# Prompt retention of a two-layer decoder step: four key blocks against all later queries, or two chunks of 256 tokens joined by a partial state

## The chip, the cores and the metric

The kernel runs on one core of one Trainium2 chip. The metric is the device time of one execution in microseconds (us). The time before is 2185.27 us, the median of 3 runs (2183.65 to 2187.77). Engines are named as in the profile: PE is TensorE, DVE is VectorE, ACT is ScalarE, POOL is GpSimd, SP is SyncE, whose queue starts nearly all DMA transfers.

## The reference, cut to what matters

Each of two layers projects 512 prompt tokens and 64 sample tokens, runs a retention mixer of 4 heads (256 wide) and a pooling mixer of 4 groups, and projects the result out. The change lies in the retention of the prompt, which the reference computes by chunks, with a state S between them:

```python
def retention_chunk(qc, kc, vc, S, log_g):
    ...
    scores = jnp.einsum('bqhd,bkhd->bhqk', qc, kc) * dmask[None]
    intra = jnp.einsum('bhqk,bkhe->bqhe', scores, vc)
    q_decay = jnp.exp((idx + 1.0)[:, None] * log_g[None, :])
    inter = jnp.einsum('bqhd,bhde->bqhe', qc, S) * q_decay[None, :, :, None]
    k_decay = jnp.exp((C - 1.0 - idx)[:, None] * log_g[None, :])
    S_new = jnp.exp(C * log_g)[None, :, None, None] * S + jnp.einsum(
        'bkhd,bkhe->bhde', kc * k_decay[None, :, :, None], vc)
    return intra + inter, S_new
```

The chunk length does not change the result. The final state of each head is an output (new_ret_p, 256 KB per head).

## The kernel before, in words

All large products are made in three passes: an operand is split into a high and a low part (`split`, L89: ACT casts the high part at L91, DVE subtracts it at L92), and `mm3` (L116) issues high x high, high x low and low x high as L117, L118 and L119.

One layer's `in_phase` (L497) runs `head(h)` for h = 0 to 3 (L588) and then four `pool_group`s (L706). In layer one it lies at about 286 to 700 us of the span, in layer two at about 1369 to 1780 us; a head takes some 72 us. Everywhere in it PE has one filler: `columns()` (L500) computes pairs of 128-row column blocks of the input projection by `gemm` (L130). Such a gemm is 48 matmuls of 288 columns (L137) into two PSUM tiles named `acc`; the pool has four `acc` tiles, so the gemm after the next reuses the tiles of this one, and may start when DVE has added them to `part` (L512, two instructions per gemm, one per tile). The weights of a gemm come as a 1 MB transfer `raw` (L103, SP, two buffers) and are split by L91 and L92.

In a head, q and k are rotated and split, v is transposed to token-major (`token_major`, L570, transposes L577). Then, for each block j of 128 keys, the scores of all queries that may see it go into a `pb` tile (L625), DVE multiplies by the decay mask (L629), the product is split (L631), and six matmuls add it into the outputs `po[0]`, `po[1]` (L633). The width n is 512, 384, 256 and 256 columns for j = 0 to 3, because the start column is `min(j, 2) * P`. ACT copies the outputs out (L637). Then comes the part of the 64 sample tokens: `retention_state` (L375) loads 8 states of 256 KB, four of them into the ring `s0_ring` of four buffers (L380, L379), and its first matmul (L385) waits for all four loads of its group; L402 and L403 update and store these states. Head normalisation follows: `rsqrt` (L311), whose last PE step spreads a row over partitions (L327), whose copy is L328, and the multiplications L668. Only then is the final prompt state made: k is transposed with decay (L670), 24 matmuls of 256 columns (L674) fill `sf`, ACT copies it to `so`, a buffer of `s0_ring` (L676, L677), and SP stores it (L678). The gate multiplies the head's result (L681); `block_sums` (L190 to L193) and splits (L92) prepare operands that POOL's queue writes out and, from L698, reads back (`m<-operand`).

A pool group works on DVE with window scans (L730) and their corrections (L732 to L737), multiplies gates (L528) and scales (L750).

The order of instructions on each engine is set by the scheduler when the kernel is built; each engine then runs its list in that order, and semaphores hold an instruction until its inputs and buffers are ready.

Of the kernel before, what the change touches and what calls it, by code (L numbers as in the profile page):

```python
# [8 lines left out]
F32R = mybir.dt.float32r  # L9
I32 = mybir.dt.int32  # L10
AF = mybir.ActivationFunctionType
ALU = mybir.AluOpType
PSUM = bass.MemoryType.PSUM

P = 128
L = 2
KT = 16
NP = 512
# [6 lines left out]
DK = 256  # L25
# [13 lines left out]
def decoder_kernel(ctx: ExitStack, tc: tile.TileContext, a, decay8):  # L39
    nc = tc.nc  # L40
# [20 lines left out]
    def tmp():  # L61
        return buf("tmp")
# [53 lines left out]
    def mm3(out, wh, wl, xh, xl, start, stop, **kw):  # L116
        nc.tensor.matmul(out, wh, xh, start=start, stop=False, **kw)  # L117
        nc.tensor.matmul(out, wh, xl, start=False, stop=False, **kw)  # L118
        nc.tensor.matmul(out, wl, xh, start=False, stop=stop, **kw)  # L119
# [4 lines left out]
    def mix_tile():  # L124
        return ps.tile([P, 512], F32, tag="po", name="po", bufs=2)

    def bank(shape):
        return ps.tile(list(shape), F32, tag="pb", name="pb", bufs=2)
# [233 lines left out]
    consts = {}  # L362
# [134 lines left out]
    def in_phase(l, raws, r2, rB, cos, sin):  # L497
        b_ring, st_ring, rot_ring, s0_ring = Ring(0, 12), Ring(12, 4), Ring(16, 8), Ring(24, 4)
# [89 lines left out]
        def head(h):  # L588
            ident = consts["ident"]
            mask = buf("mask", (P, 640))  # L590
            nc.sync.dma_start(out=mask, in_=a["mask_p"][:, h])
            q = rotary(8 + h)
            qs = split_prompt(q)
# [7 lines left out]
            k = rotary(12 + h)  # L601
# [6 lines left out]
            vt = token_major(v)  # L608
# [8 lines left out]
            nc.scalar.copy(vs, tp[:, :DK])  # L617

            po = [mix_tile() for _ in range(2)]
            for j in range(4):  # L620
                c0 = min(j, 2) * P
                n = NP - c0
                sp = bank((P, 512))
                for dt in range(2):
                    mm3(sp[:, :n], ks[dt][0][:, j * P:(j + 1) * P], ks[dt][1][:, j * P:(j + 1) * P],  # L625
                        qs[dt][0][:, c0:], qs[dt][1][:, c0:], dt == 0, dt == 1)
                m0 = c0 - j * P + P
                sm = tmp()
                nc.vector.tensor_tensor(out=sm[:, :n], in0=sp[:, :n], in1=mask[:, m0:m0 + n], op=ALU.mult)  # L629
                sth, stl = st_ring.tile((P, NP), F32R), st_ring.tile((P, NP), F32R)  # L630
                split(sth[:, :n], stl[:, :n], sm[:, :n])  # L631
                for e in range(2):
                    mm3(po[e][:, c0:], vt[j][0][:, e * P:(e + 1) * P], vt[j][1][:, e * P:(e + 1) * P],  # L633
                        sth[:, :n], stl[:, :n], j == 0, j == 3)
            o = [rot_ring.tile() for _ in range(2)]
            for e in range(2):
                nc.scalar.copy(o[e][:, :NP], po[e])  # L637
# [29 lines left out]
            for e in range(2):  # L667
                nc.vector.tensor_tensor(out=o[e], in0=o[e], in1=ro, op=ALU.mult)  # L668

            kt = token_major(k, scale=consts["kdec"][:, h])  # L670
            sf = bank((P, 2, DK))
            for dt in range(2):
                for j in range(4):
                    mm3(sf[:, dt], kt[j][0][:, dt * P:(dt + 1) * P], kt[j][1][:, dt * P:(dt + 1) * P],  # L674
                        vt[j][0], vt[j][1], j == 0, j == 3)
            so = s0_ring.tile((P, 2, DK))  # L676
            nc.scalar.copy(so, sf)  # L677
            nc.sync.dma_start(out=a["new_ret_p"][l, h].rearrange("(t p) e -> p t e", p=P), in_=so)  # L678

            for i, g in enumerate(silu_gates(20 + h)):  # L680
                nc.vector.tensor_tensor(out=o[i], in0=o[i], in1=g, op=ALU.mult)  # L681
# [2 lines left out]
            both = buf("x", (P, 2, HN), F32R)  # L684
# [71 lines left out]
        for h in range(NH):  # L756
            head(h)
# [178 lines left out]
def _tables(np):  # L936
    f = np.float32
    half = DK // 2
    inv = (10000.0 ** (-(np.arange(half, dtype=f) / f(half))).astype(np.float64)).astype(f)
    pos = np.concatenate([np.arange(NP), 4096 + np.tile(np.arange(NS), NB)]).astype(f)  # L940
    ang = (inv[:, None] * pos[None, :]).astype(np.float64)
    lg = np.log(f(1.0) - f(2.0) ** (f(-5.0) - np.arange(NH, dtype=f))).astype(np.float64)
    sc = DK ** -0.5
    p = np.arange(P)
    d = (np.arange(640) - P)[None, :] - p[:, None]
    mask = np.where(d[:, None] >= 0, np.exp(np.maximum(d, 0)[:, None] * lg[None, :, None]) * sc, 0.0)
    tok = np.arange(64)
    t, b = tok % NS, tok // NS
    ds = t[None, :] - t[:, None]
    ok = (b[None, :] == b[:, None]) & (ds >= 0)  # L950
    mask_s = np.where(ok[:, None], np.exp(np.maximum(ds, 0)[:, None] * lg[None, :, None]) * sc, 0.0)
    kdec = np.exp((NP - 1 - (p[:, None, None] + P * np.arange(4)[None, None, :])) * lg[None, :, None]) * sc
    ones = np.ones((P, 1, 1))
    qdec_s = ones * np.exp((t[:NS] + 1)[None, :] * lg[:, None])[None]
    kdec_s = ones * (np.exp((NS - 1 - t[:NS])[None, :] * lg[:, None]) * sc)[None]
    w = np.array(WINDOWS)
    invcnt = ones * (1.0 / np.minimum(np.arange(16)[None, :] + 1, w[:, None]))[None]
    tables = {
        "cos": np.cos(ang), "sin": np.sin(ang), "ident": np.eye(P),
        "kdec": kdec, "qdec_s": qdec_s, "kdec_s": kdec_s,  # L960
        "mask_s": np.concatenate([np.zeros_like(mask_s), mask_s]), "mask_p": mask, "invcnt": invcnt,
    }
    return {k: np.ascontiguousarray(v.astype(f)) for k, v in tables.items()}, [float(np.exp(NS * g)) for g in lg]
# [63 lines left out]
```

## Time and profile before

| what | value |
|---|---|
| median of 3 runs | 2185.27 us (2183.65 to 2187.77) |
| the profiled execution's own time | 2186.74 us |
| its span | 2184.8 us |
| PE busy | 2168.9 us (99%) |
| DVE busy | 1726.2 us (79%) |
| ACT busy | 1063.6 us (49%) |
| granted TensorE clock | 9 tenths or more in every slice of 40 |

The profiled execution is 1.47 us above the median of the runs. Matmul ends in the trace are modelled and overlap the next start, so the time that a matmul takes from its successors is read from start to start.

### The profile page before, as it was taken

To read this page: it belongs to the slowest core of one execution; us is meant where nothing else is said; L and a number is where in the kernel's file an instruction comes from. 1 tells how busy PE (TensorE), PEld (TensorE's weight loads), DVE (VectorE), ACT (ScalarE), POOL (GpSimd) and SP (SyncE) were. 2 spreads that over 40 slices of the span, in tenths; PEclk is the share of its full clock that TensorE was granted. 3 is DMA by queue.
4 is the path that set the end of the run, shared out by engine and by line. 5 is a ranking of instruction groups with operands and counts; after the bars stand their busy time and mean duration, and the time that the engine had idled before them with its cause. 6 is when DMAs were issued, how large, how long until landed. Compare 5 with 4: busy or idle time off the path is not lost.

```text
span 2184.8 us, 42838 instructions
## 1 busy us (share of the span) xinstructions
PE 2168.9 (99%) x16716; PEld 2138.1 (98%) x16716; DVE 1726.2 (79%) x3186; ACT 1063.6 (49%) x2065; POOL 178.5 (8%) x210
## 2 busy tenths in 40 slices
PE   9999999999999999999999999999999999999998
PEld 9999999999999999999999999999999999999998
DVE  8788766677588998888887887667786889979865
ACT  5565534444434555655455554434443345566532
POOL 3000000000211111200110000000002111111000
PEclk9999999999999999999999999999999999999999
DMA  7455454565873333656544554456568743346564
GB/s 233 145 196 187 157 170 150 188 193 175 273 245 130 130 119 125 210 175 225 192 167 149 172 177 151 149 159 210 167 206 256 233 143 124 113 142 197 178 209 141
DMA packets 148202, 385.59 MB, mean 176 GB/s; under 512 B 15776, under 2 KB 54176, under 8 KB 127136
## 3 DMA queue, kind: packets, MB, share of 16 engines
q1 hardware_dynamic: 129168, 340.37, 47.4%
q0 software_dynamic: 18688, 42.48, 6.2%
q8 instruction: 131, 2.15, 0.4%
q14 instruction: 71, 0.58, 0.1%
q10 hardware_dynamic: 144, 0.02, 0.0%
HBM read 284.97 MB, written 97.84 MB: 175 GB/s over the span
## 4 chain that ended last, share of the span: by engine, by line
PE 90%; DVE 4%; DMA 3%; issue 1%; ACT 1%; SPq 0%; DVEq 0%; ACTq 0%
PE acc L137 34%; PE acc L119 13%; PE acc L118 13%; PE acc L117 13%; PE acc L233 3%; PE pb L118 3%; PE pb L119 3%; PE pb L117 3%; DMA x<-ple 2%; PE po L137 1%; DVE wl L92 1%; PE pb L401 1%; PE po L385 1%; PE pb L577 1%; PE po L327 1%
## 5 line engine op out<-in xcount | busy, mean ns | idle before, releaser
L137 PE MATMUL acc<-m,wh 128*128 128x288 f32 x3584 | 648.7, 296 | 0.0
L91 ACT CAST wh<-raw 128x512 fp32r<-128x512 f32 x567 | 350.5, 620 | 503.6 <-PE acc L137 263.6
L118 PE MATMUL acc<-m,wh 128*128 128x288 f32 x1944 | 573.1, 295 | 0.0
L117 PE MATMUL acc<-m,wh 128*128 128x288 f32 x1944 | 571.3, 295 | 0.9 <-ACT m L256 0.5
L119 PE MATMUL acc<-m,wl 128*128 128x288 f32 x1944 | 567.7, 295 | 0.7 <-DVE wl L92 0.7
L137 PEld LDWEIGHTS acc<-m,wh 128*128 128x128 f32 x3584 | 531.7, 188 | 7.0 <-issue 6.0
L92 DVE TENSOR_TENSOR wl<-raw,wh 128x512 fp32r<-128x512 f32 x567 | 401.7, 710 | 125.8 <-ACT wh L91 119.1
L137 PE MATMUL acc<-m,wl 128*128 128x288 f32 x1792 | 388.8, 295 | 0.0
L117 PEld LDWEIGHTS acc<-m,wh 128*128 128x128 f32 x1944 | 364.7, 188 | 2.1 <-ACT m L256 1.0
L118 PEld LDWEIGHTS acc<-m,wh 128*128 128x128 f32 x1944 | 365.0, 188 | 0.1
L119 PEld LDWEIGHTS acc<-m,wl 128*128 128x128 f32 x1944 | 362.8, 188 | 1.3 <-DVE wl L92 1.3
L91 ACT CAST wh<-S 128x512 fp32r<-128x512 f32 x356 | 220.6, 620 | 236.7 <-PE acc L118 149.7
L137 PEld LDWEIGHTS acc<-m,wl 128*128 128x128 f32 x1792 | 288.7, 188 | 1.1 <-issue 0.5
L92 DVE TENSOR_TENSOR wl<-S,wh 128x512 fp32r<-128x512 f32 x356 | 252.1, 709 | 23.6 <-ACT wh L91 22.4
L512 DVE TENSOR_TENSOR part<-acc,part 128x288 f32<-128x288 f32 x192 | 79.6, 451 | 84.2 <-PE acc L137 83.8
L246 POOL TENSOR_TENSOR S<-raw 128x512 f32<-128x512 f32 x45 | 77.9, 1732 | 650.9 <-DMA raw<-in_w_out 214.6
L246 DVE TENSOR_TENSOR S<-raw 128x512 f32<-128x512 f32 x133 | 93.5, 703 | 22.0 <-DMA raw<-in_w_in 18.0
L691 POOL DMA_DIRECT2D operand<-x x48 | 25.8, 538 | 972.1 <-ACT x L91 965.7
L118 PE MATMUL pb<-m,wh 128*128 128x288 f32 x324 | 95.5, 295 | 0.0
L119 PE MATMUL pb<-m,wl 128*128 128x288 f32 x324 | 95.2, 294 | 0.0
L117 PE MATMUL pb<-m,wh 128*128 128x288 f32 x324 | 95.1, 293 | 0.0
L256 ACT COPY d<-acc 128x288 f32<-128x288 f32 x228 | 86.3, 394 | 0.0
(280 smaller groups left out, 3388.9 us busy)
## 6 DMA issues: line engine op xcount, KB each, us to landing
raw<-in_w_in SPq DMA_DIRECT2D x95, 1024.0 KB, 5.4
raw<-in_w_out SPq DMA_DIRECT2D x32, 1024.0 KB, 5.1
raw<-in_w_gate SPq DMA_DIRECT2D x32, 1024.0 KB, 5.6
proj<-d SPq DMA_DIRECT2D x96, 288.0 KB, 2.1
part<-proj SPq DMA_DIRECT2D x96, 288.0 KB, 3.1
operand<-x POOLq DMA_DIRECT2D x56, 288.0 KB, 3.3
m<-operand POOLq DMA_DIRECT2D x56, 288.0 KB, 5.5
x<-in_x SPq DMA_DIRECT2D x36, 288.0 KB, 4.1
```

The lines of the kernel that those rows point to most:

```text
L91: nc.scalar.copy(hi, src)
L92: return nc.vector.tensor_tensor(out=lo, in0=src, in1=hi.bitcast(F32), op=ALU.subtract)
L117: nc.tensor.matmul(out, wh, xh, start=start, stop=False, **kw)
L118: nc.tensor.matmul(out, wh, xl, start=False, stop=False, **kw)
L119: nc.tensor.matmul(out, wl, xh, start=False, stop=stop, **kw)
L137: nc.tensor.matmul(acc[h], u, v[:, h * HN:(h + 1) * HN], start=(i == 0 and passno == 0), stop=(i == n - 1 and passno == 2),)
L233: nc.tensor.matmul(acc[h], w[:, j], xs[h][passno == 1], start=(i == 0 and j == 0 and passno == 0), stop=(i == 1 and j == 3 and passno == 2),)
L246: eng.tensor_tensor(out=s, in0=x, in1=y, op=op)
L256: ops["tail_act"] = nc.scalar.copy(dst, src)
L327: nc.tensor.matmul(rows[:, (q % 2) * QN:(q % 2 + 1) * QN], pick[:, q], r, start=True, stop=True)
L512: nc.vector.tensor_tensor(out=half(t, h), in0=acc[h], in1=half(t, h), op=ALU.add)
L691: nc.gpsimd.dma_start(out=operand_dram[l][7 * h + 1 + 2 * i + k], in_=part)
```

## The change

Prompt retention now works in two chunks of 256 tokens. Key blocks 0 and 1 meet only queries 0 to 255, blocks 2 and 3 only queries 256 to 511, so all four widths are 256. The partial state of keys 0 to 255 is made first (12 matmuls), copied by ACT into `so` and split; the queries of the second chunk are multiplied on DVE by a decay table, which lies in an unused part of the mask, and split; and 12 new matmuls of 256 columns add their product with the partial state to the outputs. The state of keys 256 to 511 (12 matmuls) is then added to `so` by DVE and stored. The whole making of the state therefore moves from behind the head normalisation to a place ahead of the sample part, and `so` takes its `s0_ring` buffer ahead of this head's four state loads. In the changed kernel the lines of the places below are 29 higher, and 20 higher from the gate multiplication on: L668 is L697 there, L681 is L701, L730 is L750, L678 is L663.

```diff
             po = [mix_tile() for _ in range(2)]
+            n = 2 * P
             for j in range(4):
-                c0 = min(j, 2) * P
-                n = NP - c0
+                c0 = j // 2 * n
+                cols = slice(c0, c0 + n)
...
-                        qs[dt][0][:, c0:], qs[dt][1][:, c0:], dt == 0, dt == 1)
+                        qs[dt][0][:, cols], qs[dt][1][:, cols], dt == 0, dt == 1)
...
-                    mm3(po[e][:, c0:], vt[j][0][:, e * P:(e + 1) * P], vt[j][1][:, e * P:(e + 1) * P],
-                        sth[:, :n], stl[:, :n], j == 0, j == 3)
+                    mm3(po[e][:, cols], vt[j][0][:, e * P:(e + 1) * P], vt[j][1][:, e * P:(e + 1) * P],
+                        sth[:, :n], stl[:, :n], j % 2 == 0, j == 1, skip_group_check=True)
+
+            kt = token_major(k, scale=consts["kdec"][:, h])
+
+            def state_of(js):
+                sf = bank((P, 2, DK))
+                for dt in range(2):
+                    for j in js:
+                        mm3(sf[:, dt], kt[j][0][:, dt * P:(dt + 1) * P], kt[j][1][:, dt * P:(dt + 1) * P],
+                            vt[j][0], vt[j][1], j == js[0], j == js[-1])
+                return sf
+
+            so = s0_ring.tile((P, 2, DK))
+            nc.scalar.copy(so, state_of((0, 1)))
+            s1h, s1l = (st_ring.tile((P, 2, DK), F32R) for _ in range(2))
+            split(s1h, s1l, so)
+            qb = []
+            for dt in range(2):
+                t = tmp()[:, :n]
+                nc.vector.tensor_tensor(out=t, in0=q[dt][:, n:NP], in1=mask[:, 3 * P:], op=ALU.mult)
+                both = st_ring.tile((P, 2, n), F32R)
+                split(both[:, 0], both[:, 1], t)
+                qb.append((both[:, 0], both[:, 1]))
+            for e in range(2):
+                for dt in range(2):
+                    mm3(po[e][:, n:], s1h[:, dt, e * P:(e + 1) * P], s1l[:, dt, e * P:(e + 1) * P], *qb[dt],
+                        False, dt == 1, skip_group_check=True)
+            nc.vector.tensor_tensor(out=so, in0=so, in1=state_of((2, 3)), op=ALU.add)
+            nc.sync.dma_start(out=a["new_ret_p"][l, h].rearrange("(t p) e -> p t e", p=P), in_=so)
...
-            kt = token_major(k, scale=consts["kdec"][:, h])
-            sf = bank((P, 2, DK))
-            for dt in range(2):
-                for j in range(4):
-                    mm3(sf[:, dt], kt[j][0][:, dt * P:(dt + 1) * P], kt[j][1][:, dt * P:(dt + 1) * P],
-                        vt[j][0], vt[j][1], j == 0, j == 3)
-            so = s0_ring.tile((P, 2, DK))
-            nc.scalar.copy(so, sf)
-            nc.sync.dma_start(out=a["new_ret_p"][l, h].rearrange("(t p) e -> p t e", p=P), in_=so)
...
     mask = np.where(d[:, None] >= 0, np.exp(np.maximum(d, 0)[:, None] * lg[None, :, None]) * sc, 0.0)
+    mask[:, :, 3 * P:] = np.exp((np.arange(2 * P, NP) - (NP - 1))[None, None, :] * lg[None, :, None])
```

The scheduler gives the changed kernel another order of instructions. Three places of it follow; a tile's name carries its buffer's number, so two rows with one number speak of one tile.

**PE at the end of the last head of a layer.** Before, the row spreading L327 stands near the end of a gemm (tiles acc_7921 and acc_7922):

```order
L137 MATMUL acc_7922<-m38_2490,wh_7917 128x288
L327 MATMUL po_7322<-tmp_7309,pick_63 128x144 x2
L327 MATMUL po_7326<-tmp_7309,pick_63 128x144 x2
L137 MATMUL acc_7921<-m39_2491,wh_7917 128x288
L137 MATMUL acc_7922<-m39_2491,wh_7917 128x288
```

Now, two matmuls into the next gemm (acc_8283 and acc_8284), with the gemm of acc_8198 and acc_8199 just finished; 46 matmuls later comes acc_8390, which takes the buffer of acc_8198:

```order
L137 MATMUL acc_8198<-m42_2790,wl_8195 128x288
...
L137 MATMUL acc_8199<-m42_2790,wl_8195 128x288
L137 MATMUL acc_8283<-m28_1740,wh_8273 128x288
L137 MATMUL acc_8284<-m28_1740,wh_8273 128x288
L327 MATMUL po_7484<-tmp_7471,pick_63 128x144 x2
L327 MATMUL po_7488<-tmp_7471,pick_63 128x144 x2
L137 MATMUL acc_8283<-m29_1741,wh_8273 128x288
...
L137 MATMUL acc_8284<-m42_2790,wl_8278 128x288
L137 MATMUL acc_8390<-m28_1740,wh_8382 128x288
```

So L327 has moved from behind the 32nd matmul of a gemm to behind the 2nd of one, as a count over the lists shows.

**DVE at the same place.** Before, the two additions L512 that free a finished gemm's tiles stand between the gate multiplications:

```order
L668 TENSOR_TENSOR m22_7187<-m22_7187,tmp_7299 128x576
L668 TENSOR_TENSOR m23_7188<-m23_7188,tmp_7299 128x576
L681 TENSOR_TENSOR m22_7187<-m22_7187,g_7444 128x576
L512 TENSOR_TENSOR part_7911<-acc_7921,part_7911 128x288
L681 TENSOR_TENSOR m23_7188<-m23_7188,g_7512 128x576
L512 TENSOR_TENSOR part_7911<-acc_7922,part_7911 128x288
L92 TENSOR_TENSOR wl_8162<-raw_7812,wh_8161 128x512
```

Now the same seventeen other instructions come first, and the two L512 after all of them (the middle of the list is left out):

```order
L697 TENSOR_TENSOR m22_7349<-m22_7349,tmp_7461 128x576
L697 TENSOR_TENSOR m23_7350<-m23_7350,tmp_7461 128x576
L701 TENSOR_TENSOR m22_7349<-m22_7349,g_7556 128x576
L701 TENSOR_TENSOR m23_7350<-m23_7350,g_7624 128x576
L190 TENSOR_TENSOR tmp_7628<-m22_7349 128x288
...
L752 TENSOR_TENSOR tmp_7738<-tmp_7734,c_invcnt_1050 128x16
L754 SCALAR_TENSOR_TENSOR tmp_7738<-tmp_7734,d_7728 128x496
L92 TENSOR_TENSOR wl_8548<-raw_8281,wh_8547 128x512
L512 TENSOR_TENSOR part_8188<-acc_8198,part_8188 128x288
L512 TENSOR_TENSOR part_8188<-acc_8199,part_8188 128x288
```

The release of acc_8198 has moved behind the start of the pool group's work (L750, L752 and L754 are its scan and corrections).

**SP in the last head.** Before, the store of a head's state and the load that reuses its buffer stand early in the following head (here the store of head 2, and its reuse by head 3):

```order
L506 DMA part<-proj_292 128x576
L678 DMA out_new_ret_p<-m_6466 128x2x256
L380 DMA m_7208<-in_state_ret 128x2x256
L506 DMA part<-proj_251 128x576
L103 DMA raw<-in_w_in 128x2048
```

Now head 3 stores its own state, and its own fourth state load reuses the buffer; a weight load stands ahead of the store:

```order
L380 DMA x<-in_state_ret 128x2x256 x4
L103 DMA raw<-in_w_in 128x2048
L663 DMA out_new_ret_p<-m_7293 128x2x256
L380 DMA m_7370<-in_state_ret 128x2x256
L403 DMA out_new_ret_s<-m_7364 128x2x256
```

The load of m_7370 is one of the four that L385 of the same head waits for. On PE, 76 matmuls of L137, 12 of the new product and eight small ones lie between the end of head 3's state matmuls and that L385. In heads 1 and 2 a weight load also stands ahead of the store, in head 0 none.

## Rows read from the trace of the kernel before

**Rows 1.** The page: the span, each engine's busy time (share of the span) and instructions, and the chain of waits by engine.

```profile
span 2184.8 us, 42838 instructions
PE 2168.9 (99%) x16716; PEld 2138.1 (98%) x16716; DVE 1726.2 (79%) x3186; ACT 1063.6 (49%) x2065; POOL 178.5 (8%) x210
PE 90%; DVE 4%; DMA 3%; issue 1%; ACT 1%; SPq 0%; DVEq 0%; ACTq 0%
```

**Rows 2.** Timeline of PE in head 0 of layer one, at the scores (first and third matmul of three in a row), and one stretch of plain gemm: start in us, time in us, engine, line, operation, out<-in, array, shape, count.

```profile
333.44 0.39 PE L117 MATMUL pb<-m,m 128*128 128x512 f32 x1
...
333.90 0.39 PE L119 MATMUL pb<-m,m 128*128 128x512 f32 x1
...
335.59 0.34 PE L117 MATMUL pb<-m,m 128*128 128x384 f32 x1
...
335.94 0.34 PE L119 MATMUL pb<-m,m 128*128 128x384 f32 x1
...
338.48 0.28 PE L117 MATMUL pb<-m,m 128*128 128x256 f32 x1
...
338.72 0.28 PE L119 MATMUL pb<-m,m 128*128 128x256 f32 x1
...
598.81 0.69 PE L137 MATMUL acc<-m,wh 128*128 128x288 f32 x4
599.34 0.42 PE L137 MATMUL acc<-m,wl 128*128 128x288 f32 x2
599.60 0.70 PE L137 MATMUL acc<-m,wh 128*128 128x288 f32 x4
```

**Rows 3.** Groups of DVE and ACT instructions between 286 and 700 us, shapes apart: line, engine, operation, out<-in, shape, count, then busy us and mean ns of one, then the idle time before them and what ended it.

```profile
L629 DVE TENSOR_TENSOR tmp<-pb,mask 128x512 f32<-128x512 f32 x4 | 2.8, 692 | 1.6 <-PE pb L119 1.6
L629 DVE TENSOR_TENSOR tmp<-pb,mask 128x256 f32<-128x256 f32 x8 | 3.4, 424 | 4.3 <-PE pb L119 4.3
L92 DVE TENSOR_TENSOR m<-m,m 128x512 fp32r<-128x512 f32 x16 | 10.6, 686 | 3.2 <-ACT m L91 3.2
L91 ACT CAST m<-m 128x512 fp32r<-128x512 f32 x16 | 9.9, 621 | 6.8 <-PE pb L119 5.2 <-DVE m L522 1.5
L677 ACT COPY m<-pb 128x512 f32<-128x512 f32 x4 | 2.3, 587 | 3.7 <-PE pb L119 3.4
```

**Rows 4.** Busy time of the engines in stretches: from:to, then length, and busy us (instructions) of PE, PEld, DVE, ACT and POOL, granted clock, DMA share, GB/s. The first lies in head 0, the second in head 3, the third in the pool groups.

```profile
340.00:344.00 4.00, 4.00 (x29) 3.83 (x27) 1.23 (x5) 1.56 (x4) 0.00 (x0) 1.00 0.40 83
556.00:564.00 8.00, 8.00 (x61) 7.82 (x60) 2.34 (x6) 1.72 (x5) 4.31 (x8) 1.00 0.99 329
600.00:616.00 16.00, 16.00 (x123) 16.00 (x122) 16.00 (x35) 7.20 (x12) 5.93 (x11) 1.00 0.79 248
```

**Rows 5.** Timeline of PE at the end of head 3, layer one and (last) layer two; columns as in rows 2.

```profile
597.30 1.15 PE L327 MATMUL po<-tmp,pick 128*128 128x144 f32 x8
598.19 0.52 PE L137 MATMUL acc<-m,wh 128*128 128x288 f32 x2
...
1680.79 1.15 PE L327 MATMUL po<-tmp,pick 128*128 128x144 f32 x8
```

**Rows 6.** Timeline of DVE there, layer one and (last two) layer two; in brackets the idle time before and what ended it.

```profile
598.91 1.43 DVE L668 TENSOR_TENSOR m<-m,tmp 128x576 f32<-128x576 f32 x2 [1.35 <-ACT tmp L328]
600.26 0.75 DVE L681 TENSOR_TENSOR m<-m,g 128x576 f32<-128x576 f32 x1
600.93 0.45 DVE L512 TENSOR_TENSOR part<-acc,part 128x288 f32<-128x288 f32 x1
601.30 0.75 DVE L681 TENSOR_TENSOR m<-m,g 128x576 f32<-128x576 f32 x1
...
608.93 0.82 DVE L512 TENSOR_TENSOR part<-acc,part 128x288 f32<-128x288 f32 x2
...
1682.40 1.43 DVE L668 TENSOR_TENSOR m<-m,tmp 128x576 f32<-128x576 f32 x2 [1.35 <-ACT tmp L328]
...
1692.42 0.81 DVE L512 TENSOR_TENSOR part<-acc,part 128x288 f32<-128x288 f32 x2
```

**Rows 7.** Transfers, each from a view of a short stretch: out<-in, queue, operation, count, KB each, median us from issue to landing. The first two are a state's store and the load that reuses its buffer, at 384 to 388 us; the next such a store at 528 to 534 us; then a weight load and the stores issued right behind it, at 357 to 360 us; then two state loads at 550 to 553 us; then head 3 at 555 to 566 us.

```profile
out_new_ret_p<-m SPq DMA_DIRECT2D x1, 256.0 KB, 2.6
m<-in_state_ret SPq DMA_DIRECT2D x1, 256.0 KB, 2.6
...
out_new_ret_p<-m SPq DMA_DIRECT2D x1, 256.0 KB, 4.1
...
raw<-in_w_in SPq DMA_DIRECT2D x1, 1024.0 KB, 6.5
out_new_ret_s<-m SPq DMA_DIRECT2D x2, 256.0 KB, 6.8
...
x<-in_state_ret SPq DMA_DIRECT2D x2, 256.0 KB, 6.9
...
m<-operand POOLq DMA_DIRECT2D x10, 288.0 KB, 5.5
x<-in_state_ret SPq DMA_DIRECT2D x1, 256.0 KB, 5.2
```

**Rows 8.** Timeline of PE in head 0: the small matmuls of the sample part; columns as in rows 2.

```profile
347.24 0.55 PE L646 MATMUL pb<-sts,vs 128*128 128x64 f32 x4
...
347.93 0.70 PE L137 MATMUL acc<-m,wh 128*128 128x288 f32 x4
```

## The prediction

> **What bounds the kernel now.** I read the page first. PE is busy 2168.9 of 2184.8 us, and the chain of waits is 90% PE [rows 1]: a PE matmul saved is time saved, and any wait put on PE is time lost, unless PE would have waited later anyway. DVE follows with 79%, which is an average. The table by stretches splits it: in the middle of a head DVE works 1.23 of 4 us, in head 3 it works 2.34 of 8 us, but at the start of the pool groups 16.00 of 16 us [rows 4]. So DVE work added in a head is cheap, and DVE work that is late at the end of a layer's last head is not. Then I read the PE timeline for the price of one matmul, the DVE timeline for the end of head 3, and the transfers, because the state's store moves.
>
> **PE columns (one answer: a gain).** A matmul's price is its start-to-start distance; modelled durations overlap. With 512 columns the first and third start 0.46 us apart, 0.23 each; with 384 it is 0.35, 0.175 each; with 256 it is 0.24, 0.12 each [rows 2]. A head loses 12 matmuls of 512 and 12 of 384, which become 24 of 256, and gains 12 of 256: 12 x 0.23 + 12 x 0.175 = 4.86 us become 36 x 0.12 = 4.32 us. That is 0.54 us a head, and for 8 heads **-4.3 us**. The state's 24 matmuls only move. This is small: the two spared blocks of scores and outputs are nearly paid back by the 12 new matmuls.
>
> The Trainium skill, "TensorE: Matmul & The Clock Gate", section on the back-to-back issue gap, speaks against the change: it gives about 81 ns per matmul at 128 columns and only about 131 ns at 512 in a stream of weight loads and matmuls. A straight line between these, an estimate from that page, gives 98 ns at 256 and 114 ns at 384, and the change would add 36 x 98 - 12 x 131 - 12 x 114 = 588 ns a head, +4.7 us in all. The rows here give 230 ns at 512, with as many weight loads as matmuls [rows 1, 2], so the measurement decides and wide matmuls are not cheap here.
>
> **DVE and ACT work in a head (nothing, by cover).** DVE adds one split of 512 columns (0.69), two decay multiplications and two subtractions of 256 (4 x 0.42) and the addition of the second half state (taken as 0.69, by the 512-wide multiplication): 3.05 us. It saves 0.27 twice for the 512-wide mask and split, and about half for the 384-wide: 0.8 us. Net +2.25 us a head [rows 3]. ACT gains some 1.1 us by the same rows. The cover is the 1.23 of 4 us [rows 4]; uncovered it would be 2.25 x 8 = 18 us, which I exclude since DVE is two thirds idle there. The 12 new matmuls wait for copy, cast and subtraction of the half state, 0.59 + 0.62 + 0.69 = 1.9 us [rows 3]; between lie, by the list of head 0, the other half's 12 matmuls (1.4 us) and 14 of the gemm's (1.8 us), so PE does not wait.
>
> **The end of head 3 (the main loss).** Here the moved order matters, and it is the longest term. Before, L512 frees the finished gemm's tiles 2.02 us after L668 starts (598.91 to 600.93) [rows 6]. In the list now, the two L512 for acc_8198 and acc_8199 stand behind seventeen instructions, starting with L697 (the old L668). These are the same seventeen that before lie between L668 and the two L512 at 608.93. So their time can be read off: 608.93 - 598.91 = 10.02 us, less two L512 at 0.37 (600.93 to 601.30) = 9.28 us; layer two gives the same 10.02 (1682.40 to 1692.42) [rows 6]. L668 starts 1.61 us after the first L327 (597.30 to 598.91; 1680.79 to 1682.40) [rows 5, 6], because it needs L328's copy. One L512 takes 0.45. The release is at 1.61 + 9.28 + 0.45 = **11.34 us** after L327 begins. PE meanwhile has the L327 group, 0.89 us (597.30 to 598.19) [rows 5], and 46 gemm matmuls at 0.132 (six from 598.81 to 599.60) [rows 2], 6.06 us: it reaches acc_8390, in the buffer of acc_8198, after **6.95 us**. It waits 4.4 us, and in two layers **+8.8 us**. The wait has no cover: the next instruction in PE's list is the one that waits, and all behind it are queued too. Ends: 0, if the release does not come last; 5.5 each, if casts on ACT hold one of the seventeen a microsecond more.
>
> What is late next is the pool groups' DVE work, which has no slack (16.00 of 16) [rows 4]. Its later releases come late by less, since PE has lost time as well. I take 0.5 us a layer, **+1.0 us**; ends 0 and 2 a layer.
>
> **The state's store, now ahead of L385.** In each head the fourth state load reuses `so`'s buffer, so it waits for the store to land, and L385 waits for the load. SP waits at that load too; queued behind it are weight and part loads, whose buffers are ahead of need. Quiet, store and load take 2.6 + 2.6 us; one such store took 4.1; stores right behind a weight load took 6.8; loads near head 3's operand reads took 5.2 to 6.9 [rows 7]. In head 3, by the list of SP, the weight load is just ahead of the store, and POOL's ten operand reads of 5.5 us fill the queues (DMA share 0.99) [rows 4, 7]. The chain is 0.69 for the addition, 6.8, and some 6.4: 13.9 us. PE has 76 gemm matmuls (10.0), 12 new ones (1.4) and eight small ones (0.69 for four by the stretch 347.24 to 347.93, 1.4 for eight [rows 8]): 12.8 us. L385 waits about 1 us; ends 0 (quiet: 5.9 us against 12.8) and 2.5 (another 1.5 us of queue). Two layers: **+2 us**. In head 0, without a weight load ahead, 0.69 + 4.1 + 2.6 = 7.4 us stays under the 8.2 us that I count for PE in the same way; heads 1 and 2 (9.0 and 7.8 us) I cost at nothing as long as the weight load has mostly passed; see the second rival.
>
> **Sum.** -4.3 + 8.8 + 1.0 + 2.0 = +7.5 us, on the profiled execution 2186.74 + 7.5 = 2194.2. That execution stands 1.47 above the median, so against the runs I predict 2185.27 + 7.5 = **2192.8 us**. A measurement of this kernel can tell some 0.2%, 4.4 us, from no change.
>
> **Rivals.**
> 1. *No wait at the end of head 3.* If the tiles come free before PE asks, and no load is late, only the columns count: 2185.3 - 4.3 = 2181.0, at the edge of faster. The place is the release of acc_8198, the price 4.4 us a layer, and the point is 6.95 us after L327: the seventeen instructions and one L512 would have to fit into 5.34 us after L697 starts. For it: the waits are inferred from a list, and such waits are scarce before. Against it: the same instructions took 9.28 us in both layers, and DVE was never idle among them.
> 2. *Loads late in heads 1 and 2 as well.* If the weight load goes out directly ahead of the store, the chain is 0.69 + 6.8 + 2.6 = 10.1 us against 9.0 and 7.8: waits of 1.1 and 2.3, 3.4 a layer, 6.8 in all, giving 2199.6. It decides by when the weight buffer comes free: 3 us before the store or at the same moment. For it: SP's list has that load directly ahead. Against it: the stores here took 2.6 and 4.1 before [rows 7].
> 3. *The wait is partly given back.* If PE, once late, spares waits that it has before, or the seventeen run shorter by what L668 waited, half of the losses go: about -4.3 + 6 = +1.7, 2187.
> 4. *The change does not narrow the work.* The list of head 0 shows the 48 matmuls at 256, the 12 new ones and the state made early, so I give this nothing.
>
> **How the numbers follow.** The forecast gets 0.55 (2190 to 2196 by itself), the second rival 0.22 (2197 to 2202), the third 0.15 (2184 to 2189), the first 0.08. The forecast and the second rival are slower by over 0.2%; the third is within 0.2%; of the first, at 2181.0 against a bound of 2180.9, I count 0.06 as faster and 0.02 as same. A small part of the forecast, 0.02, falls under the bound of 2189.6. Faster 0.06, same 0.19, slower 0.75. The range leaves out the first rival and the upper end of the second: 2184.5 to 2201.
>
> **What would show it.** Right: in the new trace, PE idles about 4.4 us before an L137 some 7 us after the last head's L327 in each layer, ended by DVE's L512; DVE starts L697 about 1.6 us after L327 and is busy without a gap until then. Score and output matmuls all stand at 0.12. DVE is still idle for much of a head. L385 of head 3 waits about 1 us for a load, of heads 0 to 2 for nothing. Wrong: PE gaps at L385 in heads 1 and 2, a gap at the 12 new matmuls, or a PE timeline without the gap after L327.

## The result: 20 us slower, and the profile after

| what | before | after |
|---|---|---|
| median, 6 runs each | 2185.28 us (2183.65 to 2188.31) | 2205.64 us (2200.28 to 2211.8) |
| ratio | | 1.0092 (95%: 1.0079 to 1.0106) |
| profiled execution, own time | 2186.74 us | 2204.03 us |

The forecast was 2192.8 us with a range up to 2201: the sign was right, the size 12.8 us too small. The page of the changed kernel, against [rows 1]:

```profile
span 2202.3 us, 43090 instructions
PE 2168.7 (98%) x16812; PEld 2142.3 (97%) x16812; DVE 1736.2 (79%) x3234; ACT 1066.4 (48%) x2089; POOL 179.5 (8%) x210
PE 82%; DMA 7%; DVE 5%; issue 4%; ACT 1%; SPq 0%; POOL 0%; DVEq 0%; ACTq 0%; POOLq 0%
```

PE's busy time is the same to 0.2 us, though its matmuls stream fewer columns, and the span is 17.5 us longer. The chain of waits has moved from PE (90% to 82%) to DMA, DVE and issue. So PE waits, and some of its matmuls take longer.

PE's timeline in the last head, both layers, answers to [rows 5] (start, time, engine, line, operation, tiles, array, shape, count, idle time before and what ended it):

```profile
580.97 0.56 PE L137 MATMUL acc<-m,wh 128*128 128x288 f32 x3
584.52 1.93 PE L385 MATMUL po<-m,u 128*32 128x256 f32 x16 [2.99 <-DMA m<-in_state_ret]
586.20 1.75 PE L385 MATMUL po<-x,u 128*32 128x256 f32 x16
587.88 0.40 PE L137 MATMUL acc<-m,wh 128*128 128x288 f32 x1
...
615.48 1.14 PE L327 MATMUL po<-tmp,pick 128*128 128x144 f32 x8
...
622.31 0.42 PE L137 MATMUL acc<-m,wl 128*128 128x288 f32 x2
626.98 0.82 PE L137 MATMUL acc<-m,wh 128*128 128x288 f32 x2 [4.24 <-DVE part L512]
627.60 0.44 PE L137 MATMUL acc<-m,wl 128*128 128x288 f32 x1
627.84 0.68 PE L137 MATMUL acc<-m,wh 128*128 128x288 f32 x2
...
1676.80 1.07 PE L385 MATMUL po<-m,u 128*32 128x256 f32 x16 [1.97 <-issue]
...
1706.40 1.14 PE L327 MATMUL po<-tmp,pick 128*128 128x144 f32 x8
...
1717.90 0.82 PE L137 MATMUL acc<-m,wh 128*128 128x288 f32 x2 [4.25 <-DVE part L512]
```

Two waits stand in each layer: one before L385 of head 3 (start to start 3.28 and 2.27 us, so some 3.15 and 2.14 us over the usual distance of 0.13), one before the L137 that reuses acc_8198's buffer, 11.5 us behind the first L327 (4.4 us each). And behind the second, one matmul takes 0.24 us (627.60 to 627.84) instead of 0.132.

DVE's timeline at the second wait, against [rows 6]:

```profile
617.09 1.43 DVE L697 TENSOR_TENSOR m<-m,tmp 128x576 f32<-128x576 f32 x2 [0.55 <-ACT tmp L328]
...
626.38 0.81 DVE L512 TENSOR_TENSOR part<-acc,part 128x288 f32<-128x288 f32 x2
```

L697 starts 1.61 us after L327 and the two L512 9.29 us after L697, as worked out (1.61 and 9.28).

The table by stretches shows what the clock did (length; busy us and instructions of PE, PEld, DVE, ACT, POOL; granted clock; DMA share; GB/s):

```profile
585.00:586.00 1.00, 1.00 (x16) 0.59 (x12) 0.00 (x0) 0.00 (x0) 0.00 (x0) 0.50 0.00 0
...
624.00:626.00 2.00, 0.00 (x0) 0.00 (x0) 2.00 (x6) 1.24 (x2) 0.98 (x2) 0.79 1.07 423
630.00:632.00 2.00, 2.00 (x10) 2.00 (x10) 1.73 (x6) 0.24 (x1) 1.54 (x3) 0.50 1.16 359
632.00:634.00 2.00, 2.00 (x17) 2.00 (x17) 1.43 (x2) 0.43 (x1) 0.80 (x2) 1.00 1.02 215
...
1676.50:1679.00 2.50, 2.20 (x34) 1.47 (x35) 1.14 (x2) 0.15 (x1) 0.00 (x0) 1.00 0.00 0
```

PE stands still, the granted clock falls from 1.00 (2.4 GHz) to 0.50 (1.2 GHz), and stays there for some microseconds after PE works again: 10 instructions in 2 us at half clock, 17 at full. The 32 L385 matmuls of head 3 take 3.36 us (584.52 to 587.88) in layer one, against 1.86 us in layer two (1676.80 to 1678.66), where the clock stood at 1.00 behind the shorter wait. The Trainium skill, "TensorE: Matmul & The Clock Gate", part 1, has the two levels and the fall after idleness; the trace agrees, at 0.50 here.

Last, the transfers of head 3, first layer one (568 to 572 us, the last row 580 to 584 us), then layer two (1660 to 1664 us, the last row 1668 to 1676 us), against [rows 7] (out<-in, queue, operation, count, KB each, median us to landing):

```profile
m<-operand POOLq DMA_DIRECT2D x6, 288.0 KB, 9.6
raw<-in_w_in SPq DMA_DIRECT2D x1, 1024.0 KB, 10.5
...
out_new_ret_p<-m SPq DMA_DIRECT2D x1, 256.0 KB, 11.4
...
m<-in_state_ret SPq DMA_DIRECT2D x1, 256.0 KB, 3.6
...
m<-operand POOLq DMA_DIRECT2D x7, 288.0 KB, 7.9
raw<-in_w_in SPq DMA_DIRECT2D x1, 1024.0 KB, 7.1
...
out_new_ret_p<-m SPq DMA_DIRECT2D x1, 256.0 KB, 8.9
...
m<-in_state_ret SPq DMA_DIRECT2D x1, 256.0 KB, 5.1
```

The state's store takes 11.4 and 8.9 us there; I had 6.8. The load that reuses its buffer, the last row of each layer, takes 3.6 and 5.1 us; I had 6.4. In layer two the profile names no releaser for the wait at L385 (`issue`), but that load was issued at 1671.61 us and landed 5.1 us later, 0.1 us before L385 starts.

**The account**, between the two profiled executions (spans 17.5 us apart): the L117 to L119 matmuls, summed from start to start over the whole trace, go from 1082.1 to 1077.9 us, -4.2. The waits behind L327 give +8.8 (2 x 4.4), those at L385 +5.3, three later waits for L512 in the pool groups +3.5 (645.08 to 646.38, 652.70 to 653.33 and 1741.43 to 1743.39 us, less 0.13 each). Two of these three hang on a `part` load for which DVE itself waits; its rows there:

```profile
645.86 0.46 DVE L512 TENSOR_TENSOR part<-acc,part 128x288 f32<-128x288 f32 x1 [1.39 <-DMA part<-proj]
...
1742.79 0.82 DVE L512 TENSOR_TENSOR part<-acc,part 128x288 f32<-128x288 f32 x2 [1.32 <-DMA part<-proj]
```

Half clock gives 1.5 (L385), 20 x 0.115 = 2.3 behind 626.98 and 12 x 0.117 = 1.4 behind 1717.90: +5.2. Together +18.6; the 1.1 us over the measured 17.5 is not traced to a place. The medians differ by 20.4, since this profiled execution is 1.6 us below its kernel's median and that of before 1.5 above.

### The profile page after: what moved, and what is told of

It reads as the page before. It is cut to its first block, busy times and chain, and to the rows that moved or that the text cites. A ratio compares the mean times of both kernels' runs of the same rounds, so it can differ in the third digit from the quotient of the medians.

```text
span 2202.3 us, 43090 instructions
## 1 busy us (share of the span) xinstructions
PE 2168.7 (98%) x16812; PEld 2142.3 (97%) x16812; DVE 1736.2 (79%) x3234; ACT 1066.4 (48%) x2089; POOL 179.5 (8%) x210
## 4 chain that ended last, share of the span: by engine, by line
PE 82%; DMA 7%; DVE 5%; issue 4%; ACT 1%; SPq 0%; POOL 0%; DVEq 0%; ACTq 0%; POOLq 0%
PE acc L137 27%; PE acc L118 13%; PE acc L117 13%; PE acc L119 13%; DMA x<-ple 4%; PE pb L119 3%; PE pb L118 3%; PE pb L117 3%; PE acc L233 3%; PE po L137 1%; DVE wl L92 1%; DVE m L882 1%; DVE x L881 1%; PE po L385 1%; DVE x L872 1%
## 5 line engine op out<-in xcount | busy, mean ns | idle before, releaser
L137 PE MATMUL acc<-m,wh 128*128 128x288 f32 x3584 | 656.6, 297 | 11.5 <-DVE part L512 11.5
L117 PE MATMUL acc<-m,wh 128*128 128x288 f32 x1944 | 571.4, 295 | 0.5 <-ACT m L256 0.5
L119 PE MATMUL acc<-m,wl 128*128 128x288 f32 x1944 | 567.4, 295 | 0.3 <-DVE wl L92 0.3
L137 PEld LDWEIGHTS acc<-m,wh 128*128 128x128 f32 x3584 | 535.9, 189 | 16.6 <-issue 13.4
L137 PE MATMUL acc<-m,wl 128*128 128x288 f32 x1792 | 401.1, 296 | 0.0
L117 PEld LDWEIGHTS acc<-m,wh 128*128 128x128 f32 x1944 | 364.6, 188 | 1.8 <-ACT m L256 1.0
L119 PEld LDWEIGHTS acc<-m,wl 128*128 128x128 f32 x1944 | 362.8, 188 | 0.8 <-DVE wl L92 0.8
L137 PEld LDWEIGHTS acc<-m,wl 128*128 128x128 f32 x1792 | 294.1, 189 | 1.3 <-issue 1.3
L512 DVE TENSOR_TENSOR part<-acc,part 128x288 f32<-128x288 f32 x192 | 79.6, 451 | 53.2 <-PE acc L137 48.6
L119 PE MATMUL pb<-m,wl 128*128 128x288 f32 x324 | 95.2, 294 | 1.5 <-DVE wl L92 1.5
L117 PE MATMUL pb<-m,wh 128*128 128x288 f32 x324 | 95.1, 293 | 0.0
```

What stands on the lines that cost most here:

```text
L137: nc.tensor.matmul(acc[h], u, v[:, h * HN:(h + 1) * HN], start=(i == 0 and passno == 0), stop=(i == n - 1 and passno == 2),)
L512: nc.vector.tensor_tensor(out=half(t, h), in0=acc[h], in1=half(t, h), op=ALU.add)
```

## The experiments

My theory, after this: the columns pay as priced, and the loss is the early state's `so` in `s0_ring`. It makes L385 wait for a store and, because the sample part and the head's end come later against the gemms, puts the head's end and the pool groups' work on DVE together, ahead of the L512 that frees PE; waits of such length then cost clock. Rival one: the added DVE and ACT work costs (2.25 us a head). Rival two: wide matmuls are cheap, so that there is nothing to gain.

**e1: so in another buffer.**

```diff
-            so = s0_ring.tile((P, 2, DK))
+            so = buf("d")[:, :2 * DK].rearrange("p (t e) -> p t e", t=2)
```

> Edit: the state buffer so comes from the ring of work buffers d, not from s0_ring; all computation is that of the changed kernel. Theory (place of so): the fourth state load no longer waits for the store of so, so L385 of head 3 has no wait (3.1 and 2.1 us go), the head's end comes earlier in the lists, the 4.4 us wait behind L327 goes in both layers, and with these waits the stretches at half clock go too. Left are the columns (-4.3) and about 1.3 us a layer of small waits for L512: 2183 to 2187 us. Rival (the added DVE and ACT work, 2.25 us a head, is what costs): the work is all still there, so the time stays near 2205, at least above 2198.

Measured: 2190.0 us (11 runs), ratio 1.0021 (1.0011 to 1.003). Three quarters of the loss went with one buffer, all the added work being still there, and in the trace no wait is left at L385 nor behind L327. The order of the matmuls shows the step between: in layer one 1874 gemm matmuls start ahead of head 3's L327 in the changed kernel, 1812 in e1 and 1760 before, so that L327 stands behind the 2nd, the 36th and the 32nd matmul of a gemm. But 2183 to 2187 was too low. PE's waits that are left in the pool groups of layer one, and the transfers at 630 to 640 us:

```profile
636.33 0.53 PE L137 MATMUL acc<-m,wh 128*128 128x288 f32 x2 [0.68 <-DVE part L512]
645.42 0.50 PE L137 MATMUL acc<-m,wh 128*128 128x288 f32 x2 [2.49 <-DVE part L512]
```

```profile
raw<-in_w_in SPq DMA_DIRECT2D x1, 1024.0 KB, 8.0
...
u<-in_state_pool SPq DMA_DIRECT2D x1, 184.0 KB, 7.9
```

The second pool group's small inputs are issued right behind a 1 MB weight load and land with it. DVE waits 2.19 us for `in_state_pool`, until 641.30, and the L512 behind that wait frees PE late. As with the state's store, a small transfer is late beside a large one, at a place I had not looked at. Behind 645.42 the clock was at half again, 15 matmuls at 0.237 (1.6 us).

**e2: the move alone, scores wide.** The whole making of the state, unsplit, stands ahead of `o`; nothing else:

```diff
+            kt = token_major(k, scale=consts["kdec"][:, h])
+            ...
+            so = s0_ring.tile((P, 2, DK))
+            nc.scalar.copy(so, sf)
+            ...
             o = [rot_ring.tile() for _ in range(2)]
```

> Edit: the kernel before with its wide scores, only with the whole making and storing of the state moved to where the change has it, so from s0_ring; no split of the state, no new matmuls, no added DVE work. Theory (the move costs): the lists again put the L512 that frees a gemm's tiles behind the last head's end; by the list it comes about 6 us late in each layer, with half clock behind it: 2185 + 12 + 4 = about 2200, 2195 to 2206. Rival (the added work costs, not the move): no work is added, so 2184 to 2188.

Measured: 2199.77 us (4 runs), ratio 1.0064 (1.0051 to 1.0078), as expected. The move costs 14 us without any added work. PE's wait, and the stretches of it and behind it:

```profile
626.42 0.82 PE L137 MATMUL acc<-m,wh 128*128 128x288 f32 x2 [6.53 <-DVE part L512]
```

```profile
619.60:626.40 6.80, 0.29 (x3) 0.06 (x2) 6.30 (x14) 2.50 (x5) 2.69 (x5) 0.89 0.97 314
626.40:631.50 5.10, 5.08 (x21) 5.10 (x22) 5.10 (x12) 1.25 (x2) 3.77 (x7) 0.50 1.14 360
```

DVE is busy through the wait (6.30 of 6.80 us), so PE waits for DVE's order, and 21 matmuls follow at half clock. This wait, its like of 6.2 us in layer two and the half clock behind both come to 18.2 us, more than the 12.4 us between the two profiled spans; where the rest is gained is not traced.

**e3: narrow columns alone.**

```diff
-                c0 = min(j, 2) * P
-                n = NP - c0
+                n = 2 * P
+                c0 = j // 2 * n
...
```

This kernel leaves out what the second chunk's queries take from the first 256 keys; it serves for the time alone.

> Edit: the kernel before, with all four widths 256 and nothing else; the second chunk's queries never meet the first 256 keys, that part of the output is left out. The state stays at its old place. Theory (columns priced from start to start): 12 x (0.23 - 0.12) + 12 x (0.175 - 0.12) = 1.98 us a head, 15.8 us in 8 heads: 2169 to 2171. Rival (wide matmuls cost little more than narrow ones, some 16 ns from 256 to 384 and 33 ns to 512): 0.6 us a head, 4.7 in all: 2180 or more.

Measured: 2171.55 us (4 runs), ratio 0.993 (0.9913 to 0.9947): 14.2 us less. From start to start, the L117 to L119 matmuls sum to 1065.5 us, 16.6 less than before; in the score, output and state matmuls alone, which hold all that the edit narrows, 69.2 against 84.9 us, 15.7 less. Rival two falls. The Trainium skill, "TensorE: Matmul & The Clock Gate", section "Back-to-back issue gap", has some 131 ns per matmul for 512 columns; the estimate from it, 4.7 us less, would have given 2180 or more, and the rows decide against it here.

**e4: the wait filled.** 32 unused matmuls between the last matmul before the wait (`last_mm`) and the one that waits:

```diff
+            if g == groups[2]:
+                fill = bank((P, 512))
+                with tc.issue_after(last_mm[0].ins):
+                    for _ in range(32):
+                        nc.tensor.matmul(fill[:, :HN], r2[1][0][:, :P], half(r2[0][0], 0), start=True, stop=True)
...
```

> Edit: the changed kernel with 32 matmuls of 288 columns, whose product nobody reads, put on PE between the last matmul before the wait behind L327 and the matmul that waits, in each layer; they need 32 x 0.132 = 4.2 us, the wait is 4.4. Theory (the slow matmuls behind the wait are the clock's, which fell because PE stood still): the wait is filled, the granted clock stays at 1.0 there, and the 20 and 12 matmuls at 0.247 us run at 0.132: 2.3 + 1.4 = 3.7 us less than the changed kernel, 2201 to 2203. Rival (they are slow because of transfers or DVE at the same place): they stay slow, 2205 to 2207. Should the filling cost time of its own, it would be 2213.

Measured: 2202.48 us (4 runs), ratio 1.0073 (1.0057 to 1.0088). PE there, and the granted clock of that stretch:

```profile
619.88 4.38 PE L734 MATMUL pb<-m,m 128*128 128x288 f32 x32
624.29 0.50 PE L139 MATMUL acc<-m,wh 128*128 128x288 f32 x2
```

```profile
626.00:628.00 2.00, 2.00 (x17) 2.00 (x16) 1.44 (x2) 0.00 (x0) 1.07 (x2) 1.00 0.47 157
```

The same matmuls, behind a wait as long but filled, run 17 in 2 us at clock 1.00, where they were 10 at 0.50. That the slowness there is the clock's is shown. The total says less: it fits 2201 to 2203, but in the trace a later wait grew to 3.04 us from start to start in layer one (1.30 in the changed kernel) and 3.00 in layer two (1.96), and behind each 25 matmuls ran at half clock. PE, earlier now, only waited later for the same DVE.

**e5: POOL's operand reads held back** until the first L385 of head 3 (`first_state`):

```diff
-                nc.gpsimd.dma_start(out=t, in_=operand_dram[l][7 * j + i])
+                after_all(nc.gpsimd.dma_start(out=t, in_=operand_dram[l][7 * j + i]), [first_state[0]])
...
```

> Edit: the changed kernel, but POOL's reads of the operands (m<-operand) wait for the first state matmul (L385) of head 3, so none of them runs while head 3's state is stored; the weight load stays right ahead of the store on SP. Behind that point the lists differ, so only the stretch up to L385 of head 3 is read. Theory (the reads make the store slow; it took 11.4 and 8.9 us): it takes 6 to 7, as stores right behind a weight load did before (6.8), the reload about 3, and the wait at L385 of head 3 is 0, at most 0.5 us. Rival (the weight load ahead is the cause): the store still takes 9 to 11 and PE still waits 2 to 3 us.

Measured: one run, 2194.15 us. The transfers at 566 to 574 us:

```profile
raw<-in_w_in SPq DMA_DIRECT2D x1, 1024.0 KB, 5.3
out_new_ret_p<-m SPq DMA_DIRECT2D x1, 256.0 KB, 4.0
m<-in_state_ret SPq DMA_DIRECT2D x1, 256.0 KB, 2.6
```

With the weight load 2.0 us ahead of the store (567.12 and 569.13 us) but no operand reads, the store took 4.0 instead of 11.4 us, the weight load 5.3 instead of 10.5, and there is no wait at L385 in either layer. In layer two of the changed kernel the weight load went 1.9 us ahead (1660.78 and 1662.65 us), and with the reads under way the store took 8.9. So the reads made it slow, more than the weight load that I had priced. The Trainium skill, "DMA: Bandwidth & Descriptors", section "Issuing engines are not separate DMA queues", says that queues of different engines share the same 16 DMA engines and interleave; 11.4 against 4.0 us agrees. That the whole run is 10 us faster than the changed kernel is not used: its lists differ behind that point.

**e6: the move alone, so elsewhere** (e2 with e1's line).

> Edit: the kernel before with the whole state made and stored early and wide scores, as in the run that moved it alone, but so comes from the ring d. Theory (the ring of so carries the loss of the move): without it no wait behind L327 and none at L385: 2185 to 2189 us. Rival (any early state delays the end of the head on DVE): as with the ring, 2197 to 2202.

Measured: 2192.6 us (4 runs), ratio 1.0035 (1.0021 to 1.0049). Half of the move's cost went with the buffer, and the waits behind L327 are gone. But 7 us stay where I expected at most 4. Its profiled execution is the quickest of the four (2190.06), and its one wait at L385, 1.04 us for a state load, does not explain them. The order of the matmuls tells more; PE in head 0, the last two rows of the kernel before:

```profile
353.21 0.28 PE L118 MATMUL pb<-m,m 128*128 128x256 f32 x1
353.42 0.62 PE L385 MATMUL po<-m,u 128*32 128x256 f32 x4
353.98 0.38 PE L119 MATMUL pb<-m,m 128*128 128x256 f32 x1
...
350.40 1.07 PE L385 MATMUL po<-m,u 128*32 128x256 f32 x16
351.40 0.51 PE L401 MATMUL pb<-u 128*128 128x256 f32 x2
```

State matmuls, which use the whole array (`128*128`), now stand among the L385 matmuls, which use 32 columns of it (`128*32`). Before, 16 of L385 in a row take 1.00 us to the next start; here four take 0.56, and the state matmul ahead of them 0.21 instead of 0.12. From start to start the L385 matmuls sum to 21.3 us over the trace, against 15.2 before, 1.3 of it at that wait. So much of the 7 us lies there, read from the trace alone: no run tested it. The gemms' matmuls sum to 6.3 us less than before in this execution, which nothing here explains.

**e7: so elsewhere, and the end of head 3 written later.** e1 and:

```diff
-            for i, g in enumerate(silu_gates(20 + h)):
+            gates = list(silu_gates(20 + h))
+            def tail():
+                for i, g in enumerate(gates):
...
+            return tail
...
         def pool_group(g, tail=None):
...
+            if tail:
+                tail()
             nc.sync.dma_start(out=a["new_pool"][l, :, 2 * g:2 * g + 2], in_=npool)
```

> Edit: so from the ring d, and the end of head 3 on DVE (gate products, block sums, splits) written behind the first pool group's inputs, so that by the lists the pool group's L512 stand ahead of it and the second group's small loads (in_w_pool, in_state_pool) go out ahead of a weight load instead of behind one. Theory (what is left in the kernel with so elsewhere, 1.0 + 2.8 and 1.0 + 2.1 us of waits for L512 and one stretch at half clock, is the pool groups' order): these go, 2181 to 2184 us. Rival (what is left is the added DVE work): 2188 to 2191.

Measured: 2183.73 us (10 runs), ratio 0.9994 (0.9984 to 1.0004), as expected: no wait over 0.5 us in the pool groups, and the clock at 1.00. All the added DVE work is still there, so rival one falls.

**e8: also the second half of the state late.** e7, and:

```diff
-            nc.vector.tensor_tensor(out=so, in0=so, in1=state_of((2, 3)), op=ALU.add)
-            nc.sync.dma_start(out=a["new_ret_p"][l, h].rearrange("(t p) e -> p t e", p=P), in_=so)
             o = [rot_ring.tile() for _ in range(2)]
...
+            nc.vector.tensor_tensor(out=so, in0=so, in1=state_of((2, 3)), op=ALU.add)
+            nc.sync.dma_start(out=a["new_ret_p"][l, h].rearrange("(t p) e -> p t e", p=P), in_=so)
             gates = list(silu_gates(20 + h))
```

> Edit: as the run before this one, and the second half of the state is made, added and stored only behind the head normalisation, where the whole state was made before; the partial state and its 12 matmuls stay early. Theory: only the columns' 4.3 us are left, no waits in heads, at most 1 us of small waits: 2181 to 2183 us, faster than both kernels. Rival (the added DVE work shows in the pool groups): 2186 or more.

Measured: **2178.91 us** (8 runs), ratio 0.9974 (0.9963 to 0.9984): faster than both kernels. Its page and the pool groups' stretches, against the row of 600 to 616 us in [rows 4]:

```profile
span 2178.4 us, 43090 instructions
PE 2164.5 (99%) x16812; PEld 2140.9 (98%) x16812; DVE 1741.8 (80%) x3234; ACT 1067.7 (49%) x2089; POOL 179.3 (8%) x210
```

```profile
600.00:620.00 20.00, 20.00 (x153) 20.00 (x152) 18.70 (x39) 9.51 (x16) 4.84 (x9) 1.00 0.58 180
620.00:640.00 20.00, 20.00 (x153) 20.00 (x152) 16.90 (x39) 6.85 (x14) 3.78 (x7) 1.00 1.07 359
```

DVE has more work than in the changed kernel (1741.8 us), and PE does not wait there. The gain over before, 6.5 us by the medians, is 2 more than I expected; the L117 to L119 matmuls sum to 6.1 us less than before, 3.9 of it in the score, output and state matmuls. Most of the 4.8 us against e7 lies where e6 lost time: L385 sums to 15.5 us here, to 18.7 in e7, where matmuls of L401 (whole array) stand more often between those of L385; those of L401 sum to 1.5 us less here.

**e9, a control: the late end of head 3 in the kernel before**, nothing else.

> Edit: the kernel before with nothing but the late end of head 3 (gate products, block sums and splits written behind the first pool group's inputs); wide scores, state at its old place, so from s0_ring. Theory (the late end only takes away waits that the changed kernel has, the gain of the best kernel is the columns'): the kernel before has no wait there, so no change, 2184 to 2187 us. Rival (the late end is itself what makes the best kernel faster): 2177 to 2182.

Measured: 2184.82 us (11 runs), ratio 0.9998 (0.9988 to 1.0007). No change: the late end by itself gains nothing. That e8's gain is the chunks' fits this and the 3.9 us above; the kernel before with only `so` in another buffer was not run.

**e10: e8 without the late end of head 3.**

> Edit: the best kernel without the late end of head 3: narrow columns, partial state early, second half of the state made, added and stored behind the normalisation, so from the ring d. By its list on SP the second pool group's small loads stand right behind a weight load, as in the kernel with so elsewhere. Theory (that place costs waits for L512 of 0.6 + 0.6 us a layer by the list, more if the small loads land as late as there, 7.9 us): 2182 to 2187 us, slower than the best kernel by 3 to 8. Rival (the late end of head 3 is without effect): 2178 to 2180.

Measured: 2186.3 us (12 runs), ratio 1.0002 (0.9993 to 1.0012), 7.4 us above e8. PE's waits in layer one, and the transfers at 628 to 640 us:

```profile
636.75 0.54 PE L137 MATMUL acc<-m,wh 128*128 128x288 f32 x2 [2.24 <-DVE part L512]
644.68 0.50 PE L137 MATMUL acc<-m,wh 128*128 128x288 f32 x2 [1.31 <-DVE part L512]
```

```profile
raw<-in_w_in SPq DMA_DIRECT2D x1, 1024.0 KB, 8.4
...
u<-in_state_pool SPq DMA_DIRECT2D x1, 184.0 KB, 8.4
```

What DVE waits for, in layer one and (last) layer two:

```profile
636.24 0.82 DVE L512 TENSOR_TENSOR part<-acc,part 128x288 f32<-128x288 f32 x2 [1.63 <-DMA part<-proj]
...
1724.86 0.36 DVE L742 TENSOR_TENSOR u<-part,long 128x64 f32<-128x64 f32 x2 [2.31 <-DMA u<-in_state_pool]
```

The first wait hangs on a `part` load; the second in layer one (DVE waits 1.02 us ahead of it) and the longest in layer two hang on `in_state_pool`, which lands with the weight load. Start to start, its waits over 0.45 us in the pool groups are 2.53, 1.60, 0.82 and 2.89 us, 7.3 us over the usual distance: the whole difference to e8 by the medians.

## Why the prediction was right or wrong

- **Columns, -4.3.** Right: -4.2 in the changed kernel, -4.5 in the score, output and state matmuls alone, the new ones included (84.9 to 80.4 us). Kernels with the same wide matmuls (before, e2, e6, e9) sum to 1081.9 to 1083.9 us, so the first figure is good to some 2 us. e3 fits the price: 15.7 us less in the matmuls that it narrows, 15.8 worked out.
- **DVE and ACT work in a head at nothing.** Right: e7 and e8 have it all and are not slower than before.
- **The end of head 3, +8.8.** Right in place, size and working: 4.4 us in each layer, L697 at 1.61 us behind L327, the release 9.29 us plus one L512 behind that. Adding up a DVE list from the same instructions of before was exact. Why the list came out so I had not asked. e1 shows it is the place of `so`: with it in `s0_ring`, more gemm matmuls go ahead of the head's sample part and end (1874 instead of 1812 ahead of L327), and L327 falls at the start of a gemm.
- **What is late next, +1.0.** Too small: 3.5 us, and only in part for the reason given. I had put it down to DVE's work; two of the three waits, 3.0 of the 3.5 us, come behind a `part` load that DVE waits for. e1 and e10 show waits of the same kind behind small loads, most of them landing with a weight load.
- **The state's store, +2.** The step that failed in its size: 5.3 us. I priced the store by the row of stores behind a weight load, 6.8, and put the operand reads on the reload only. They ran while the store did, and it took 11.4 and 8.9 (e5: 4.0 without them). The reload took 3.6 and 5.1 instead of 6.4, which by luck hid part of this: 0.69 + 11.4 + 3.6 and 0.69 + 8.9 + 5.1, less the 12.8 us of PE, are 2.9 and 1.9 us, close to the waits measured. The upper end, 2.5 a layer, was passed in layer one (3.15).
- **The clock: no term at all, +5.2.** This is the step that was missing. The trace before has no such wait in this part of the program, so no row there showed what follows one, and I priced a wait at its own length. Three of the four large waits cost 1.4 to 2.3 us more.
- Together: 2.5 (later waits) + 3.3 (store) + 5.2 (clock) = 11.0 of the 12.8 us by which the median was missed. Against the profiled execution, from which these were read, the miss is 9.8 us (2204.03 against 2194.2). Neither remainder is traced to a place.
- **Rivals.** The first (no wait at the end of head 3) and third (given back) did not come. The second, loads late in heads 1 and 2, did not either: those heads show no wait at L385, though it had the time that came nearest, 2199.6.

## What to carry to other kernels

A buffer that is taken early from a ring puts a store and a reload on the path of whoever uses the ring next; give such a tile a buffer with a later next user. Price a small transfer by all that every queue has under way while it runs, not only by what stands ahead of it on its own queue. And where PE is kept waiting for some microseconds, reckon with half clock for the matmuls behind it as well: 1.4 to 2.8 us on top here where it came, which was not behind every such wait.

## What the runs showed of the hardware

The granted clock fell to 0.50 behind waits of 3.15 (layer one, L385) and 4.4 us, but not behind one of 2.14 (layer two, L385); in e1 it fell behind a wait of 2.65 and not behind one of 1.95, in e5 behind one of 2.49, in e10 behind neither 2.4 nor 2.76. In e8 it fell behind one of 1.91, between the layers (PE starts again at 1088.97 us; some 16 matmuls at 0.24 us follow). So the length of a wait alone does not tell what follows it. How long the slow stretch lasted differed too: 20 matmuls behind one wait of 4.4 us, 12 behind the other.

From a matmul on the whole array to one on 32 columns of it the starts lay 0.21 us apart in e6 (353.21 to 353.42), against 0.12 between matmuls on the whole array with the same 256 columns.
